# One decoder layer on one core: the first weight block and x^T arrive in fewer, larger transfers, and TensorE warms up with nine matmuls

## The chip, the core and the metric

The kernel runs on one core of a Trainium2 chip. The metric is device time in microseconds (us), from the start to the end of one execution; of several runs the median is given.

## What is computed

A decoder layer for 256 tokens of width 1024, in float32. Cut to what matters:

```python
proj = jnp.einsum('bsd,de->bse', x, w_in[l])                 # 1024 -> 3072
dq, dk, dv, mq, mk, mv = jnp.split(proj, splits, axis=-1)
a_out = diff_attention(dq, dk, dv, diff_lambda[l], diff_subln_g[l], lambda_init, cos, sin)
b_out = moba_attention(mq, mk, mv, cos, sin)
mix = jnp.einsum('bse,ed->bsd', jnp.concatenate([a_out, b_out], axis=-1), w_o[l])
x = layer_norm(ALPHA * x + mix, ln1_g[l], ln1_b[l])
g, u = jnp.split(jnp.einsum('bsd,df->bsf', x, w_ffn_in[l]), 2, axis=-1)
x = layer_norm(ALPHA * x + jnp.einsum('bsf,fd->bsd', jax.nn.silu(g) * u, w_ffn_out[l]), ln2_g[l], ln2_b[l])
```

## The kernel before

All weights stream through the core once, as 49 units of 1 MB: a unit is a tile of 128 partitions by 4 blocks of 512 columns. Six pairs of units belong to the input projection, four units to the output projection, 22 and 11 to the two layers of the FFN. A unit is loaded on SyncE's queue (SP) into `raw`, then split: ScalarE (ACT) rounds it to float32r into `hi` (L190 for unit 0, L106 for later ones), and VectorE (DVE) subtracts, `lo = raw - hi` (L192, L108; one piece of units 2 to 9 goes to GpSimd). x^T, eight blocks of 128 partitions by 256 tokens, is split in the same way into `xTh` and `xTl` (L178, L179). Each product of the projections is then three matmuls on TensorE (PE): hi by hi (L142), `xTl` by hi (L143) and `xTh` by lo (L144).

The projection walks over eight blocks of the contraction, block k of x^T with block k % 4 of unit 0 (k below 4) or unit 1 (k from 4). For one block, four output slices `pj_0` to `pj_3` take three matmuls of 256 columns each, 12 in all. So 48 matmuls need unit 0 and the first four blocks of x^T, and the next 48 need unit 1 and the last four.

The order of the start is written out by hand: the transfers in L182 to L189, the casts and subtractions in the loop at L190 to L192. While nothing has landed, PE runs WARM matmuls of 512 columns on a zeroed tile (L154). The loads of units 1 to 3 come behind it, in four pieces each (L95). SP issues one transfer after another, and a transfer whose completion counter is still in use by the eighth transfer before it waits for that one. Within these lists the tool that builds the program sets each engine's own order, so a change of the start can shift instructions further down.

```python
for i in range(4):
    nc.scalar.copy(hi[0][:, i, :], raw[0][:, i, :])
    split_x(i, i + 1, nc.vector.tensor_copy if i == 0 else nc.scalar.copy)
    nc.vector.tensor_sub(lo[0][:, i, :], raw[0][:, i, :], hi[0][:, i, :].bitcast(F32))
```

Of the kernel before, what the change touches and what calls it, by code (L numbers as in the profile page):

```python
# [27 lines left out]
ALPHA = 2.0 ** 0.25  # L28
LAMBDA0 = 0.8 - 0.6 * math.exp(-0.3 * 0)
EPS = 1e-5  # L30
WARM = 7


LOAD_PIECES = {1: 4, 2: 4, 3: 4, 4: 4, 5: 4, 6: 2, 7: 2}
# [22 lines left out]
def hybrid_layer_kernel(ctx, tc, xT, xr, w_in, w_o, w_f1, w_f2, cols, rows, lamb, rot, tri, out):  # L57
    nc = tc.nc
# [11 lines left out]
    units = []  # L70
# [11 lines left out]
    raw, hi, lo = {}, {}, {}  # L82
# [69 lines left out]
    wps = psB.tile([P, 512], F32, tag="b", name="wps")  # L152
    for i in range(WARM):
        nc.tensor.matmul(wps, warm[:, :P], warm, start=True, stop=True)  # L154
# [15 lines left out]
    def load_x(a, b):  # L170
        nc.sync.dma_start(xTr[:, a:b, :], xT[:, a:b, :])

    def load_w0(i):
        nc.sync.dma_start(raw[0][:, i, :], units[0][:, i, :])

    def split_x(a, b, copy=nc.scalar.copy):
        s = slice(a, b)
        copy(xTh[:, s, :], xTr[:, s, :])  # L178
        nc.vector.tensor_sub(xTl[:, s, :], xTr[:, s, :], xTh[:, s, :].bitcast(F32))  # L179

    load_w0(0)
    load_x(0, 1)  # L182
    load_x(1, 2)
    load_w0(1)
    load_x(2, 4)
    load_w0(2)
    load_w0(3)
    load_x(4, 8)
    for i in range(4):  # L189
        nc.scalar.copy(hi[0][:, i, :], raw[0][:, i, :])  # L190
# [648 lines left out]
```

## Time and profile before

| | |
|---|---|
| median of 3 runs | 315.06 us (314.43 to 316.19) |
| the profiled execution | 314.95 us |
| its span, first to last instruction | 313.2 us |
| busy share: PE, DVE, ACT, GpSimd | 96%, 81%, 57%, 12% |
| mean granted TensorE clock | 0.991 |

The span is what the trace covers; 1.75 us of the execution lie around it. Times in the rows below count from the span's start. A PE that counts as busy is not at its peak, since a matmul's recorded length overlaps the next one; the pace is the distance between two starts. An engine's idle time costs something only where the chain that ends last goes through it.

### The profile page before, as it was taken

Reading aid. Unit: us, or ns where it says so; the run is one execution under the profiler, and the core shown is the slowest. Engines: PE = TensorE matmul, PEld = TensorE weight load, DVE = VectorE, ACT = ScalarE, POOL = GpSimd, SP = SyncE. Lnnn points to the kernel's source line nnn. Section 1 sums busy time; section 2 is a strip of 40 time slices with the busy share of each in tenths; the row PEclk is TensorE's granted clock in tenths of the full one; section 3 lists DMA queues with packets and bytes.
Section 4 is the critical chain, followed back from the end, with each engine's and each line's share of the span. In section 5 each row is a group of like instructions: output and inputs, shape, how many; then the busy total and the mean of one; then the engine's idle time right before and its main releaser. Section 6 shows DMA issues by size and latency. Waiting matters only on the chain.

```text
span 313.2 us, 4707 instructions
## 1 busy us (share of the span) xinstructions
PE 300.7 (96%) x1726; PEld 256.2 (82%) x1726; DVE 254.3 (81%) x475; ACT 177.6 (57%) x346; POOL 36.3 (12%) x38
## 2 busy tenths in 40 slices
PE   8899899999999999999999999999999999999990
PEld 5799789867887788888888888888888888888880
DVE  3799999999977189939587797597778799897975
ACT  4767479488686228337367477457747665546000
POOL 1066653310030010200000000000000000000011
PEclk9999999999999999999999999999999999999996
DMA  6989943433466450576834744654561317642011
GB/s 185 375 287 340 422 173 136 134 137 134 135 213 218 186 190 19 191 330 222 314 105 165 268 148 143 248 194 151 195 223 47 134 41 282 215 157 113 0 67 67
DMA packets 13749, 57.17 MB, mean 183 GB/s; under 512 B 1664, under 2 KB 2432, under 8 KB 8864
## 3 DMA queue, kind: packets, MB, share of 16 engines
q1 hardware_dynamic: 13440, 54.79, 50.0%
q0 software_dynamic: 288, 2.10, 1.8%
q8 instruction: 13, 0.21, 0.3%
q14 instruction: 8, 0.07, 0.1%
HBM read 55.84 MB, written 1.05 MB: 182 GB/s over the span
## 4 chain that ended last, share of the span: by engine, by line
PE 76%; DVE 12%; DMA 4%; issue 3%; POOL 1%; ACT 1%; SPq 1%; DVEq 0%; ACTq 0%
PE fc L601 21%; PE foc L683 13%; PE fc L602 11%; PE fo L683 4%; DVE lo L108 4%; DMA raw<-in_w_in_dram 4%; PE wo L142 3%; PE fr L143 2%; PE fr L142 2%; PE wo L144 2%; PE wo L143 2%; PE fr L144 2%; PE pj L142 2%; PE pj L144 2%; PE pj L143 2%
## 5 line engine op out<-in xcount | busy, mean ns | idle before, releaser
L108 DVE TENSOR_TENSOR lo<-raw,hi 128x512 fp32r<-128x512 f32 (+2 forms) x108 | 105.5, 1001 | 21.4 <-ACT hi L106 21.3
L106 ACT CAST hi<-raw 128x512 fp32r<-128x512 f32 (+2 forms) x116 | 90.2, 826 | 21.9 <-PE wo L144 9.9
L601 PE MATMUL fc<-x1T,hi 128*128 128x512 f32 x288 | 100.1, 392 | 0.0
L602 PE MATMUL fc<-x1T,lo 128*128 128x256 f32 x288 | 80.5, 280 | 0.0
L601 PEld LDWEIGHTS fc<-x1T,hi 128*128 128x128 f32 x288 | 54.1, 188 | 11.9
L602 PEld LDWEIGHTS fc<-x1T,lo 128*128 128x128 f32 x288 | 54.0, 188 | 0.0
L142 PE MATMUL pj<-xTh,hi 128*128 128x256 f32 x128 | 36.7, 294 | 1.4 <-ACT hi L190 1.4
L144 PE MATMUL pj<-xTh,lo 128*128 128x256 f32 x128 | 36.0, 288 | 0.6 <-DVE lo L108 0.5
L143 PE MATMUL pj<-xTl,hi 128*128 128x256 f32 x128 | 36.5, 287 | 0.0
L604 ACT COPY v<-fc 128x256 f32<-128x256 f32 x36 | 13.3, 370 | 23.7 <-PE fc L602 23.6
L142 PEld LDWEIGHTS pj<-xTh,hi 128*128 128x128 f32 x128 | 24.3, 193 | 2.9 <-ACT hi L190 2.5
L144 PEld LDWEIGHTS pj<-xTh,lo 128*128 128x128 f32 x128 | 24.3, 193 | 1.3 <-DVE lo L108 0.7
L143 PEld LDWEIGHTS pj<-xTl,hi 128*128 128x128 f32 x128 | 24.6, 193 | 0.1
L605 DVE TENSOR_TENSOR v<-v,fc 128x256 f32<-128x256 f32 x36 | 15.0, 418 | 9.7 <-ACT v L604 9.6
L512 POOL TENSOR_TENSOR rsf<-rsf,mhalf 128x1 f32<-128x1 f32 x2 | 1.8, 924 | 175.8 <-DVE rsf L511 175.8
L683 PE MATMUL foc<-lo,hTh 128*128 128x512 f32 x52 | 20.5, 395 | 0.0
L683 PE MATMUL foc<-hi,hTl 128*128 128x512 f32 x52 | 20.5, 394 | 0.0
L683 PE MATMUL foc<-hi,hTh 128*128 128x512 f32 x52 | 20.5, 394 | 0.0
L108 POOL TENSOR_TENSOR lo<-raw,hi 128x512 fp32r<-128x512 f32 x8 | 13.8, 1720 | 20.4 <-ACT hi L106 20.4
L284 ACT ACTIVATE E<-E,negm 128x128 f32<-128x128 f32 (+1 forms) x32 | 14.2, 445 | 2.5 <-DVE negm L281 2.4
L247 POOL TENSOR_TENSOR sh<-sh,cs_sb 128x256 f32<-128x256 f32 (+1 forms) x12 | 13.3, 1124 | 18.2 <-DVE sh L245 17.5
L142 PE MATMUL pj<-hi,xTh 128*128 128x512 f32 x32 | 13.7, 428 | 0.0
(189 smaller groups left out, 553.3 us busy)
## 6 DMA issues: line engine op xcount, KB each, us to landing
raw<-in_w_f_dram SPq DMA_DIRECT2D x28, 1024.0 KB, 5.2
raw<-in_w_in_dram SPq DMA_DIRECT2D x24, 256.0 KB, 5.4
raw<-in_w_in_dram SPq DMA_DIRECT2D x4, 1024.0 KB, 6.3
raw<-in_w_o_dram SPq DMA_DIRECT2D x4, 1024.0 KB, 4.8
raw<-in_w_f_dram SPq DMA_DIRECT2D x10, 256.0 KB, 3.8
raw<-in_w_f_dram SPq DMA_DIRECT2D x5, 512.0 KB, 5.1
raw<-in_w_in_dram SPq DMA_DIRECT2D x4, 512.0 KB, 8.7
rows<-in_rows_dram POOLq DMA_DIRECT2D x2, 1024.0 KB, 6.6
```

The lines of the kernel that those rows point to most:

```text
L106: nc.scalar.copy(h[:, s, :], r[:, s, :])
L108: eng.tensor_sub(l[:, s, :], r[:, s, :], h[:, s, :].bitcast(F32))
L142: nc.tensor.matmul(ps, sh, mh, start=first, stop=False)
L143: nc.tensor.matmul(ps, sh, ml, start=False, stop=False)
L144: nc.tensor.matmul(ps, sl, mh, start=False, stop=last)
L247: nc.gpsimd.tensor_mul(sh, sh, sin2[:, :m, :])
L284: nc.scalar.activation(e, e, AF.Exp, bias=negm[g][:, i, u : u + 1], scale=-1.0, accum_out=ls[g][:, i, u : u + 1])
L601: nc.tensor.matmul(ps, hi[u][:, i, ws], x1T[:, k], start=k == 0, stop=False)
L602: nc.tensor.matmul(ps[:, 0, :], lo[u][:, i, ws], x1T[:, k, 0, :], start=False, stop=k == KT - 1)
L604: nc.scalar.copy(v, ps[:, 1, :])
L605: nc.vector.tensor_add(v, v, ps[:, 0, :])
L683: nc.tensor.matmul(bank[name] if ps is None else ps, x, w[:, cs], start=key not in opened, stop=last and (m, i) == (len(todo) - 1, 2))
```

## The change

Unit 0 is loaded in two transfers of two blocks (512 KB) instead of four of one block (256 KB). x^T comes in pieces of 2, 2 and 4 blocks instead of 1, 1, 2 and 4. The order is weight, x, weight, x, x. WARM goes from 7 to 9. The casts and subtractions keep their sizes and their order in the source.

```diff
-WARM = 7
+WARM = 9
...
-    def load_w0(i):
-        nc.sync.dma_start(raw[0][:, i, :], units[0][:, i, :])
+    def load_w0(a, b):
+        nc.sync.dma_start(raw[0][:, a:b, :], units[0][:, a:b, :])
...
-    load_w0(0)
-    load_x(0, 1)
-    load_x(1, 2)
-    load_w0(1)
+    load_w0(0, 2)
+    load_x(0, 2)
+    load_w0(2, 4)
     load_x(2, 4)
-    load_w0(2)
-    load_w0(3)
     load_x(4, 8)
```

SP, the start of the program. `raw_101` (now `raw_103`) is unit 0, the next two `raw` tiles are units 1 and 2. Before:

```order
L174 DMA raw_101<-in_w_in_dram 128x512
L171 DMA xTr<-in_xT_dram 128x256 x2
L174 DMA raw_101<-in_w_in_dram 128x512
L171 DMA xTr<-in_xT_dram 128x512
L174 DMA raw_101<-in_w_in_dram 128x512 x2
L171 DMA xTr<-in_xT_dram 128x1024
L95 DMA raw_139<-in_w_in_dram 128x512 x4
L95 DMA raw_144<-in_w_in_dram 128x512 x4
```

Now:

```order
L174 DMA raw_103<-in_w_in_dram 128x1024
L171 DMA xTr<-in_xT_dram 128x512
L174 DMA raw_103<-in_w_in_dram 128x1024
L171 DMA xTr<-in_xT_dram 128x512
L171 DMA xTr<-in_xT_dram 128x1024
L95 DMA raw_138<-in_w_in_dram 128x512 x4
L95 DMA raw_143<-in_w_in_dram 128x512 x4
```

Five transfers stand ahead of unit 1 where eight stood; the bytes are the same.

DVE, the start of the program. `lo_103` (now `lo_105`) belongs to unit 0. Before:

```order
L178 CAST xTh<-xTr 128x256
L192 TENSOR_TENSOR lo_103<-raw_101,hi_102 128x512
L179 TENSOR_TENSOR xTl<-xTr,xTh 128x256 x2
L192 TENSOR_TENSOR lo_103<-raw_101,hi_102 128x512
L179 TENSOR_TENSOR xTl<-xTr,xTh 128x256 x2
L192 TENSOR_TENSOR lo_103<-raw_101,hi_102 128x512 x2
L179 TENSOR_TENSOR xTl<-xTr,xTh 128x512 x2
```

Now:

```order
L189 TENSOR_TENSOR lo_105<-raw_103,hi_104 128x512
L178 CAST xTh<-xTr 128x256
L189 TENSOR_TENSOR lo_105<-raw_103,hi_104 128x512
L179 TENSOR_TENSOR xTl<-xTr,xTh 128x256 x2
L189 TENSOR_TENSOR lo_105<-raw_103,hi_104 128x512 x2
L179 TENSOR_TENSOR xTl<-xTr,xTh 128x256 x2
L179 TENSOR_TENSOR xTl<-xTr,xTh 128x512 x2
```

The first cast of x^T now stands behind the first subtraction of unit 0, and the first `xTl` behind the second one. ACT's order changes alike: both casts of a pair of weight blocks now stand ahead of the x block, then the second pair, then the next two x blocks.

PE, the first matmuls on unit 1 (`hi_186` and `lo_187`, now `hi_185` and `lo_186`). Before:

```order
L142 MATMUL pj_3_185<-xTh,hi_186 128x256
L143 MATMUL pj_3_185<-xTl,hi_186 128x256
L144 MATMUL pj_0_182<-xTh,lo_187 128x256
L144 MATMUL pj_1_183<-xTh,lo_187 128x256
L144 MATMUL pj_2_184<-xTh,lo_187 128x256
```

Now:

```order
L142 MATMUL pj_0_181<-xTh,hi_185 128x256
L143 MATMUL pj_0_181<-xTl,hi_185 128x256
L144 MATMUL pj_0_181<-xTh,lo_186 128x256
L142 MATMUL pj_1_182<-xTh,hi_185 128x256
L143 MATMUL pj_1_182<-xTl,hi_185 128x256
```

Before, eight matmuls on `hi` ran ahead of the first on `lo`; now the first on `lo` is the third.

## Rows read from the trace of the kernel before

**Rows 1.** The page's busy time and chain that ended last, whole span.

```profile
PE 300.7 (96%) x1726; PEld 256.2 (82%) x1726; DVE 254.3 (81%) x475; ACT 177.6 (57%) x346; POOL 36.3 (12%) x38
...
PE 76%; DVE 12%; DMA 4%; issue 3%; POOL 1%; ACT 1%; SPq 1%; DVEq 0%; ACTq 0%
```

**Rows 2.** The chain in order of time, first 20 us: start us, us, what.

```profile
3.53 6.57 DMA raw<-in_w_in_dram
10.12 6.01 DMA raw<-in_w_in_dram
```

**Rows 3.** Timeline of PE, first 14 us: start us, us, engine, line, operation, idle before.

```profile
1.19 3.17 PE L154 MATMUL wps<-warm 128*128 128x512 bf16 x7 [1.19 <-DVE tbl L150]
...
4.32 1.19 PE L142 MATMUL pj<-xTh,hi 128*128 128x256 f32 x4
...
6.75 0.41 PE L143 MATMUL pj<-xTl,hi 128*128 128x256 f32 x1
...
7.12 0.28 PE L142 MATMUL pj<-xTh,hi 128*128 128x256 f32 x1
7.24 0.28 PE L143 MATMUL pj<-xTl,hi 128*128 128x256 f32 x1
...
10.12 0.39 PE L142 MATMUL pj<-xTh,hi 128*128 128x256 f32 x1 [1.42 <-ACT hi L190]
...
13.20 0.33 PE L142 MATMUL pj<-xTh,hi 128*128 128x256 f32 x1
```

**Rows 4.** Busy time by stretch; the last numbers are granted clock, DMA share, GB/s.

```profile
5.00:10.00 5.00, 3.70 (x23) 3.42 (x22) 2.12 (x5) 2.29 (x5) 0.00 (x0) 1.00 0.83 258
10.00:15.00 5.00, 4.88 (x39) 4.81 (x40) 4.28 (x7) 4.22 (x9) 0.00 (x0) 1.00 1.05 392
```

**Rows 5.** Timeline of SP's queue, first 15 us: issues of transfers.

```profile
0.74 0.37 SPq L174 DMA_DIRECT2D raw<-in_w_in_dram  x1
1.17 0.89 SPq L171 DMA_DIRECT2D xTr<-in_xT_dram  x2
...
4.48 9.97 SPq L95 DMA_DIRECT2D raw<-in_w_in_dram  x12
```

**Rows 6.** Transfers 1, 3, 4, 5, 7, 8, 9: KB, us from issue to landing.

```profile
raw<-in_w_in_dram SPq DMA_DIRECT2D x1, 256.0 KB, 2.8
...
xTr<-in_xT_dram SPq DMA_DIRECT2D x1, 128.0 KB, 3.3
...
raw<-in_w_in_dram SPq DMA_DIRECT2D x1, 256.0 KB, 3.6
...
xTr<-in_xT_dram SPq DMA_DIRECT2D x1, 256.0 KB, 5.2
...
raw<-in_w_in_dram SPq DMA_DIRECT2D x1, 256.0 KB, 6.6
...
xTr<-in_xT_dram SPq DMA_DIRECT2D x1, 512.0 KB, 7.4
...
raw<-in_w_in_dram SPq DMA_DIRECT2D x1, 256.0 KB, 7.6
```

**Rows 7.** Timeline of ACT, first casts of a weight block and of x^T.

```profile
3.57 0.62 ACT L190 CAST hi<-raw 128x512 fp32r<-128x512 f32 x1 [1.33 <-DMA raw<-in_w_in_dram]
...
5.01 0.41 ACT L178 CAST xTh<-xTr 128x256 fp32r<-128x256 f32 x1 [0.82 <-DMA xTr<-in_xT_dram]
```

**Rows 8.** Timeline of DVE, its first three operations on data.

```profile
3.88 0.29 DVE L178 CAST xTh<-xTr 128x256 fp32r<-128x256 f32 x1 [2.74 <-DMA xTr<-in_xT_dram]
4.22 0.69 DVE L192 TENSOR_TENSOR lo<-raw,hi 128x512 fp32r<-128x512 f32 x1
4.83 0.42 DVE L179 TENSOR_TENSOR xTl<-xTr,xTh 128x256 fp32r<-128x256 f32 x1
```

**Rows 9.** Timeline of PE, 30 to 40 us: two waits for DVE.

```profile
34.33 0.39 PE L144 MATMUL pj<-xTh,lo 128*128 128x256 f32 x1 [0.52 <-DVE lo L108]
...
39.17 0.38 PE L143 MATMUL s<-l,h 64*128 64x256 f32 x1 [0.45 <-DVE l L254]
```

## The prediction

> **What bounds the kernel now.** I read the page first. PE is busy for 96% of the span, and three quarters of the chain that ended last are PE's [rows 1]. So what the start of the kernel gives to PE, and what is not lost again before PE takes over for good, comes out of the time one for one. The chain in order of time says what the start hangs on: from 3.53 to 16.13 us it is nothing but weight transfers [rows 2]. The timeline of PE shows the same from its side [rows 3]: seven warming matmuls from 1.19 to 4.36, the first real matmul at 4.32, a hole of 1.42 us that ends at 10.12 when block 2 of unit 0 has been cast, and the first matmul on unit 1 at 13.20. Behind that PE waits for DVE at 34.33 (0.52 us) and at 39.17 (0.45 us) [rows 9]; between 5 and 10 us it stands for 1.30 us in 5 [rows 4].
>
> The pace of PE in rows 3 needs a word. Seven matmuls of 512 columns start 0.42 apart (3.17 us for all, the last one's tail included), which is 1.2 GHz; 256 columns at that level take 0.21. From about 7.0 us on, 256 columns take 0.12, which is 2.4 GHz. So the rise came 5.8 us after PE's first matmul, and PE had been at work almost without a break until then. The granted clock of these stretches reads 1.00 throughout [rows 4], so the rise is read from the pace alone.
>
> The transfers: SP issues one every 0.47 us, from 0.74 on, and reaches unit 1 at 4.48 [rows 5]. The times to landing grow from 2.8 to 7.6 us [rows 6], so the pieces land at 3.54 (block 0 of unit 0), 4.97 (x 1; x 0 a little over 3.8, since DVE casts it at 3.88 [rows 8]), 5.7 (block 1), 7.8 (x 2 and 3), 10.1 (block 3), 11.4 (x 4 to 7) and 12.1 (first piece of unit 1). The rate is 258 GB/s between 5 and 10 us and 392 from 10 to 15 [rows 4]. The start is short of bytes, and bytes move slower there than later.
>
> **The change, part by part.** The bytes and all compute instructions stay, but for two warming matmuls. What changes is when blocks land, and in which order ACT and DVE take them.
>
> *Issues.* Five transfers instead of eight stand ahead of unit 1. By 0.47 us each they are issued at 0.74, 1.2, 1.7, 2.1 and 2.6, and unit 1 follows at 3.1 instead of 4.48. SP loses nothing by it.
>
> *First weight pair, 512 KB.* Its first half cannot be used before the second has landed. Landing: not before 3.54 + 0.67 = 4.2, which is the landing of 256 KB plus another 262 kB at 392 GB/s; not after 4.97, when the same number of bytes had landed before in three pieces. I take 4.3, near the fast end, because it is one transfer and not three. The Trainium skill, page "DMA: Bandwidth & Descriptors", section "Anatomy of one DMA — SWDGE (gpsimd) path", speaks against this part: the completion fires only when the last byte has landed, after about 2.0 us and the bytes at 436 GB/s. That would put the pair at 0.74 + 2.0 + 1.2 = 3.9 and a single block at 3.3, an estimate from that page, where the trace has 3.54 for the single block. By it the first real matmul would come at 5.6 and not at the 6.0 worked out below, two more matmuls would be done by 7.0, and the end would be 0.2 us earlier.
>
> *x 0 and 1, 256 KB.* 4.3 plus 0.75 (between 0.67 at 392 GB/s and 1.02 at 258) is 5.05; bounds 4.9 and 5.7.
>
> *ACT.* A cast of a weight block takes 0.62, of an x block 0.41 [rows 7]. Blocks 0 and 1: 4.34 to 4.96 to 5.58; x 1: to 5.99.
>
> *DVE.* This is where the new order costs. The cast of x 0 stands behind the first subtraction, the first `xTl` behind the second. A subtraction takes 0.69, with starts 0.61 apart (4.22 to 4.83), an `xTl` 0.42, the cast 0.29 [rows 8]. From 4.98: `lo` 0 to 5.63, x 0 cast to 5.93, `lo` 1 to 6.55, `xTl` 0 to 6.95, `xTl` 1 to 7.35.
>
> *PE.* The first real matmul at 5.98, against 4.32. The nine warming matmuls end at 1.19 + 9 x 0.427 = 5.03, so the two that are added lie in a wait and cost nothing; they would cost up to 0.85 us only if data were there at 4.2, which the landing above excludes. PE stands still for about 0.95 us. The four matmuls on `xTh` run to 6.83, the next waits for `xTl` 0 until 7.0. If the clock is up by then, the remaining 8 of block 0 take 0.95 and the 12 of block 1 1.43: 9.4.
>
> *Second weight pair and x 2 and 3.* 512 KB more at 258 GB/s are 2.03: 7.1. Bounds 6.2 (392 GB/s) and 10.1 (when block 3 landed before). x 2 and 3 one more 1.02: 8.1. ACT casts blocks 2 and 3 from 7.1 to 8.4, x 2 and 3 to 9.2. DVE, behind it, has `xTl` 2 and 3 by about 9.5 and 9.9. PE comes at 9.4 and finds block 2 nearly ready, then block 3: 24 matmuls at 0.12 are 2.86, so unit 0 is done at 12.3, against 13.20. In other words: at 7.0 PE has done 4 matmuls where it had done 12, which puts it 0.95 behind at the fast pace; in return the hole of 1.42 and smaller halts of 0.45 (from 7.0 to 13.20, less the hole and 36 matmuls at 0.12) go. That is 0.9.
>
> *x 4 to 7 and unit 1.* At 258 GB/s x lands at 10.1 (bounds 8.2, and 11.4 as before), the first piece of unit 1 at 10.9 (8.9 and 12.1). DVE subtracts x 4 to 7 to about 12.05 and the first `lo` of unit 1 to 12.7. In the new order the third matmul on unit 1 needs it, at 12.3 + 0.24, so PE waits 0.15 there. **Net 0.75 us.**
>
> *Afterwards.* The transfers of units 1 and 2 are about 1.1 us earlier, and with them ACT and DVE, so PE's waits for DVE at 34 and 39 us stay about as long as they were: DVE's lead over PE grows by 0.3 at most, and I count nothing. DVE and GpSimd take some subtractions and shuffles up to 80 us in another order; with no row for that I bound it by half a wait of rows 9 either way, 0.25, and take nothing.
>
> The sum, against the profiled execution: 314.95 - 0.75 = **314.2**. The median of the runs shown is 315.06, 0.11 higher.
>
> **The rivals.**
>
> *The clock comes up late (slower).* PE's work is broken for about 1 us just before the rise. If the rise is then as far behind the new beginning as it was behind the first, 5.8 us, it comes at 11.8. Block 0 ends at 8.7 (8 matmuls at 0.213 from 7.0), block 1 at 11.3, 2 matmuls more at 11.8, 10 at 0.12 to 13.0, block 3 at 14.4. That is 1.2 us later than 13.20: **316.1**. It decides from the point where PE's hole is long enough to undo the seven or nine warming matmuls; against it speaks that a hole of 1.42 us at 8.7 did not bring the slow pace back [rows 3], though that was after the rise. The Trainium skill, page "TensorE: Matmul & The Clock Gate", section "Why this matters for your kernels", asks for unbroken work until the clock is up; the trace agrees with it so far, since the rise followed 5.8 us of nearly unbroken work.
>
> *The whole load runs at the later rate (faster).* If the 258 GB/s came from many small transfers, and the larger ones run at 392, the second pair lands at 6.2, x 4 to 7 at 8.2, unit 1 at 8.9. PE is then held by its own start alone: unit 0 at 12.3 as before, but no wait for `lo` (0.9 gained), and DVE is over 1 us further ahead of PE than now, which takes away the two waits of rows 9, 0.97: 314.95 - 1.87 = **313.1**.
>
> *Hidden anyway.* If x 4 to 7 still land at 11.4, DVE's stream is where it was; PE is 0.9 us early on unit 0 and waits 0.9 longer for `lo` of unit 1 or at 34 us: **315.0**. For it: the chain of rows 2 is all transfers, and the bytes are the same.
>
> **How the numbers follow.** My forecast 0.43, the late clock 0.22, the full rate 0.20, hidden 0.15. About 0.5% (1.6 us) is what a measurement of this kernel can tell from no change. Only the full rate reaches that on the fast side: nearly all of its 0.20, and 0.03 of the forecast's edge, 0.23. On the slow side the late clock gives 1.2 and needs 0.4 more, from a first pair at 4.97 or the new order further down: 0.10. The rest, 0.67, is within. The range goes from 312.8, the full rate with 0.25 for the order further down, to 316.2, the late clock.
>
> **What would show it.** Right: first transfer landed at about 4.3, first real matmul near 6.0 with a hole of about 1 us before it, no hole around 9 us, the pace of 0.12 from about 7 us, the first matmul on unit 1 near 12.3. The late clock: a pace of 0.21 beyond 9 us. The full rate: near 390 GB/s between 5 and 10 us. Hidden: the matmul on unit 1 early, and longer waits for DVE behind it. My forecast is wrong if the first pair lands after 5 us or if PE is not done with unit 0 before 13.2.

## The result, and the profile of the changed kernel

The changed kernel takes 318.71 us (median of 4 executions, 318.07 to 319.00) against 315.04 us (4 executions, 314.43 to 316.19): 1.0107 times as long, 95% interval 1.0079 to 1.0135. The forecast was 314.2 with a range to 316.2, so the prediction was wrong, in sign too. The profiled execution took 318.52 us with a span of 316.7: 3.5 us more span than before.

Its page, busy time and the chain that ended last, beside [rows 1]:

```profile
PE 301.4 (95%) x1728; PEld 256.0 (81%) x1728; DVE 253.3 (80%) x475; ACT 177.5 (56%) x346; POOL 35.1 (11%) x38
...
PE 79%; DVE 12%; issue 2%; ACT 2%; DMA 2%; POOL 1%; SPq 0%; DVEq 0%; ACTq 0%; POOLq 0%
```

PE's busy sum rose by 0.7 us only; the time in which it stood grew from 12.5 to 15.3 us. Transfers went from 4% of the chain to 2%: it leaves them at 8.7 us now and at 16.1 before, so the start hangs less on them, as meant. Yet PE's timeline of the start (columns as in [rows 3]) reads:

```profile
1.19 4.02 PE L154 MATMUL wps<-warm 128*128 128x512 bf16 x9 [1.19 <-DVE tbl L150]
6.59 0.71 PE L142 MATMUL pj<-xTh,hi 128*128 128x256 f32 x4 [1.38 <-ACT xTh L178]
7.43 0.38 PE L143 MATMUL pj<-xTl,hi 128*128 128x256 f32 x1
...
10.20 0.39 PE L142 MATMUL pj<-xTh,hi 128*128 128x256 f32 x1
11.04 0.38 PE L143 MATMUL pj<-xTl,hi 128*128 128x256 f32 x1 [0.45 <-DVE xTl L179]
...
13.86 0.28 PE L142 MATMUL pj<-xTh,hi 128*128 128x256 f32 x1
```

The first real matmul starts at 6.59 after a hole of 1.38 us, not at 5.98 after 0.95. The fast pace is there at once (four matmuls in 0.71 us), and the hole ahead of block 2 is all but gone. Unit 1 begins at 13.86, 0.66 later than the 13.20 of [rows 3], where the sum had it at 12.3. The transfers of these blocks (KB, us from issue to landing) are issued on SP at 0.74, 1.18, 1.65 and 2.11:

```profile
raw<-in_w_in_dram SPq DMA_DIRECT2D x1, 512.0 KB, 4.1
...
xTr<-in_xT_dram SPq DMA_DIRECT2D x1, 256.0 KB, 5.0
...
raw<-in_w_in_dram SPq DMA_DIRECT2D x1, 512.0 KB, 7.0
...
xTr<-in_xT_dram SPq DMA_DIRECT2D x1, 256.0 KB, 7.3
```

So they land at 4.9, 6.2, 8.7 and 9.4. ACT's casts of the weight pairs show it (beside [rows 7]), and SP's row shows when unit 1 joins in (beside [rows 5]):

```profile
4.90 1.14 ACT L187 CAST hi<-raw 128x512 fp32r<-128x512 f32 x2 [2.66 <-DMA raw<-in_w_in_dram]
...
8.70 1.14 ACT L187 CAST hi<-raw 128x512 fp32r<-128x512 f32 x2 [2.14 <-DMA raw<-in_w_in_dram]
```

```profile
3.43 10.27 SPq L95 DMA_DIRECT2D raw<-in_w_in_dram  x12
```

**Where the 3.5 us are.** I laid each matmul of the changed kernel beside the same one of the kernel before, by its place in PE's stream, and took the difference of their starts, called the lag here. It is +0.6 from 14 to 32 us, between -0.1 and +0.5 to 57 us, +1.2 from 58 to 65 us (a longer wait for `E`, the probabilities of the first attention; it is given back) and +0.55 from 66 to 70 us. At 71 us it jumps to +1.90, and from 74 us on it is +3.4 to the end. So some 0.55 is lost ahead of 70 us. It is not simply the start's 0.6 carried along: that is made up by 34 us, and at 38.80 PE waits 0.62 us for ACT's cast `h`, where it waited 0.06 before. Nearly all the rest is lost in one place of 4 us, where the last projection pieces and the first scores of the second attention meet. PE's timeline there:

```profile
70.41 0.40 PE L144 MATMUL pj<-hi,xTl 128*128 128x512 f32 x1
71.85 0.35 PE L142 MATMUL s<-h,h 64*128 64x256 f32 x1 [1.05 <-DVE negm L278]
72.37 0.38 PE L143 MATMUL s<-l,h 64*128 64x256 f32 x1 [0.16 <-DVE l L251]
...
73.69 0.80 PE L142 MATMUL pj<-hi,xTh 128*128 128x512 f32 x1
74.28 0.63 PE L143 MATMUL pj<-lo,xTh 128*128 128x512 f32 x1
...
75.99 0.63 PE L144 MATMUL pj<-hi,xTl 128*128 128x512 f32 x1
76.55 0.59 PE L142 MATMUL s<-h,h 64*128 64x256 f32 x2
```

The kernel before goes through the same instructions without a wait and without a slow stretch:

```profile
69.85 0.40 PE L144 MATMUL pj<-hi,xTl 128*128 128x512 f32 x1
70.18 0.38 PE L142 MATMUL s<-h,h 64*128 64x256 f32 x1
70.46 0.38 PE L143 MATMUL s<-l,h 64*128 64x256 f32 x1
...
71.79 0.51 PE L142 MATMUL pj<-hi,xTh 128*128 128x512 f32 x1
...
73.39 0.39 PE L142 MATMUL s<-h,h 64*128 64x256 f32 x2
```

Two losses can be read off. From the last projection matmul to the second score matmul 1.96 us go by (70.41 to 72.37) where it was 0.61 (69.85 to 70.46): 1.35 us of **waiting**. Then six matmuls of 512 columns take 2.86 us (73.69 to 76.55) where they took 1.60, and the scores behind them lose another 0.23: 1.5 us of **slow pace**. The windows of PE say what this pace is; the number after the five engines' busy times is the granted clock, which is 1.00 here in the kernel before:

```profile
72.00:73.00 1.00, 0.78 (x5) 0.38 (x5) 1.00 (x6) 0.89 (x5) 0.00 (x0) 1.00 1.08 131
73.00:74.00 1.00, 1.00 (x8) 0.88 (x9) 1.00 (x6) 0.83 (x4) 0.00 (x0) 0.84 0.87 369
74.00:77.00 3.00, 3.00 (x10) 1.96 (x11) 3.00 (x17) 2.55 (x13) 0.00 (x0) 0.50 0.43 183
77.00:78.00 1.00, 1.00 (x12) 0.84 (x11) 1.00 (x2) 0.90 (x5) 0.00 (x0) 0.95 0.00 0
```

It is 0.50, the 1.2 GHz level, through 74 to 77 us and a little on both sides, right behind the place where PE had stood.

**Why PE waits there.** The score matmul at 71.85 waits until DVE has read earlier scores (it takes the negated row maximum, `negm`, from them), the one at 72.37 for `l`. `h` and `l` are the rounded part and the remainder of the queries and keys, as `hi` and `lo` are of the weights. On DVE `negm` and `l` both stand behind the rope (the rotation of queries and keys by their position) of projection 3's second half, which begins with a shuffle. DVE in the kernel before, from the first half's rope addition on:

```profile
62.91 0.68 DVE L251 TENSOR_TENSOR a<-a,sh 128x512 f32<-128x512 f32 x1
63.51 1.28 DVE L108 TENSOR_TENSOR lo<-raw,hi 128x512 fp32r<-128x512 f32 x2
64.71 0.68 DVE L254 TENSOR_TENSOR l<-a,h 128x512 fp32r<-128x512 f32 x1
...
65.32 0.73 DVE L245 STREAM_SHUFFLE sh<-pj 128x512 f32<-128x512 f32 x1
...
69.73 0.68 DVE L254 TENSOR_TENSOR l<-a,h 128x512 fp32r<-128x512 f32 x1
```

And in the changed kernel:

```profile
63.47 0.68 DVE L248 TENSOR_TENSOR a<-a,sh 128x512 f32<-128x512 f32 x1
64.07 0.68 DVE L108 TENSOR_TENSOR lo<-raw,hi 128x512 fp32r<-128x512 f32 x1
64.89 0.69 DVE L251 TENSOR_TENSOR l<-a,h 128x512 fp32r<-128x512 f32 x1
65.72 0.69 DVE L108 TENSOR_TENSOR lo<-raw,hi 128x512 fp32r<-128x512 f32 x1
66.61 0.69 DVE L108 TENSOR_TENSOR lo<-raw,hi 128x512 fp32r<-128x512 f32 x1 [0.20 <-ACT hi L106]
...
67.23 0.74 DVE L242 STREAM_SHUFFLE sh<-pj 128x512 f32<-128x512 f32 x1
...
71.63 0.68 DVE L251 TENSOR_TENSOR l<-a,h 128x512 fp32r<-128x512 f32 x1
```

From the shuffle to `l` it is 4.41 us before and 4.40 now. From the addition to the shuffle it was 2.41 us and is now 3.76, 1.35 more, which is PE's loss: before, `l` was done at 70.41 and PE took it at 70.46, so there was no slack. A third subtraction stands ahead of the shuffle (0.61), and DVE halts three times, 0.22, 0.23 and 0.28 us beyond the 0.60 between starts, each time until a cast of ACT ends (the first at 64.24 + 0.62 = 64.86). ACT is late because its order changed too. Before, it did a weight cast at 60.76, while the addition was not ready; now that cast stands behind the cast `h` of the addition's result, and ACT idles instead:

```profile
60.76 0.62 ACT L106 CAST hi<-raw 128x512 fp32r<-128x512 f32 x1 [0.60 <-PE pj L144]
63.67 0.62 ACT L253 CAST h<-a 128x512 fp32r<-128x512 f32 x1 [2.29 <-DVE a L251]
```

```profile
64.24 0.62 ACT L250 CAST h<-a 128x512 fp32r<-128x512 f32 x1 [2.91 <-DVE a L248]
```

Nothing in the source changed there. The tool that builds the program sets each engine's order, and with the first weight blocks arriving as a pair it set DVE, ACT and GpSimd differently in some 40 places between about 17 and 93 us.

### The profile page after: what moved, and what is told of

It reads as the page before. It is cut to its first block, busy times and chain, and to the rows that moved or that the text cites. A ratio compares the mean times of both kernels' runs of the same rounds, so it can differ in the third digit from the quotient of the medians.

```text
span 316.7 us, 4704 instructions
## 1 busy us (share of the span) xinstructions
PE 301.4 (95%) x1728; PEld 256.0 (81%) x1728; DVE 253.3 (80%) x475; ACT 177.5 (56%) x346; POOL 35.1 (11%) x38
## 3 DMA queue, kind: packets, MB, share of 16 engines
HBM read 55.84 MB, written 1.05 MB: 180 GB/s over the span
## 4 chain that ended last, share of the span: by engine, by line
PE 79%; DVE 12%; issue 2%; ACT 2%; DMA 2%; POOL 1%; SPq 0%; DVEq 0%; ACTq 0%; POOLq 0%
PE fc L598 21%; PE foc L680 13%; PE fc L599 11%; PE fo L680 4%; DVE lo L108 4%; PE pj L142 3%; PE pj L143 3%; PE pj L144 3%; PE wo L142 2%; PE fr L143 2%; PE fr L142 2%; PE wo L143 2%; PE wo L144 2%; PE fr L144 2%; DMA raw<-in_w_in_dram 2%
## 5 line engine op out<-in xcount | busy, mean ns | idle before, releaser
L244 POOL TENSOR_TENSOR sh<-sh,cs_sb 128x256 f32<-128x256 f32 (+1 forms) x12 | 13.1, 1106 | 12.3 <-DVE sh L242 12.3
```

Of the source, the lines that this page charges most:

```text
L244: nc.gpsimd.tensor_mul(sh, sh, sin2[:, :m, :])
```

## The experiments

The theories when the first runs were sent: **A**, the order further down costs, by itself; **B**, the late start costs, and what is seen at 71 us follows from it; **C**, the order makes the wait, and the slow pace of the clock comes on top of it by a chance of the execution or from a second cause. To hold an order fixed, some kernels carry it as a table, `ORDER`, one row of instruction numbers for each of DVE, ACT and GpSimd; at the end a function ties each instruction to the one before it on its engine, without a semaphore:

```diff
+ORDER = [
+    [55, 66, 80, 91, 107, 137,
...
+    def pin_order():
...
+        for numbers in ORDER:
+            for a, b in zip(numbers, numbers[1:]):
+                tc.add_manual_dep(named[f"I-{first + b}"], f"I-{first + a}",
...
+    pin_order()
```

All results in one table. The runs of before beside them had medians of 314.90 to 315.09; the ratio is to those.

| kernel | executions | median (range), us | ratio, 95% interval |
|---|---|---|---|
| e1 new start, old order | 10 | 316.10 (315.65 to 316.54) | 1.0014 [0.9991, 1.0037] |
| e2 old start, new order | 10 | 317.02 (316.08 to 318.55) | 1.0061 [1.0037, 1.0085] |
| e3 changed kernel, hole filled | 10 | 317.69 (316.49 to 318.81) | 1.0066 [1.0038, 1.0093] |
| e4 changed kernel, 7 warming | 5 | 318.33 (317.56 to 318.88) | 1.0086 [1.0053, 1.0119] |
| e5 changed kernel, old order late | 5 | 316.16 (316.00 to 317.24) | 1.0035 [1.0004, 1.0065] |
| e6 only x 0 and 1 merged | 10 | 315.78 (315.02 to 316.95) | 1.0020 [0.9998, 1.0043] |
| e7 only second pair merged | 10 | 315.97 (314.98 to 317.56) | 1.0029 [1.0005, 1.0052] |
| e8 changed kernel, second pair split | 4 | 319.01 (318.30 to 319.09) | 1.0123 [1.0108, 1.0138] |
| e9 only two more warming | 10 | 314.92 (314.39 to 315.64) | 0.9988 [0.9966, 1.0010] |
| e10 only the late order | 11 | 317.76 (315.62 to 319.27) | 1.0061 [1.0029, 1.0092] |
| e11 one subtraction moved | 12 | 315.53 (315.15 to 317.41) | 1.0022 [0.9997, 1.0046] |
| e12 as e9, again | 12 | 315.17 (314.23 to 316.94) | 1.0012 [0.9988, 1.0037] |

(A twelfth execution of e10 took 595.71 us and is left out of its row. The recorded ratio is not the quotient of the two medians.)

The mean granted clock is on record for every execution, and helps to read the ranges. Of the 92 executions of the kernel before beside these runs, 76 took at most 315.69 us, with a mean clock of 0.991 to 0.996; 16 took over 316.5, with 0.988 to 0.990, and are 2.0 us longer in the mean. The profiles tell what this is: the clock is at 0.50 in the last microseconds of all 14, and the four with a mean of 0.990 or less (the changed kernel, e8, e10, e11) are the four in which it also fell earlier; the ten with 0.991 or more have no such fall. So I read a mean of 0.990 or less as such a fall. Where it lay only a profile tells.

### e1 and e2: start and order apart

e1 is the changed kernel with the old order of DVE, ACT and GpSimd behind the start; e2 is the kernel before with the new one. Both are the `ORDER` table above with the other kernel's numbers.

> The changed start, with VectorE, ScalarE and GpSimd tied, from the first instruction behind the start on, to the order that they had before. If the order further down costs the 3.4 us (theory A), the lag of 0.6 us that the start leaves at 14 us is taken back by about 36 us as in the changed kernel, no slow pace appears at 74 us, and the time is 314.5 to 315.5. If the late start itself costs them, because it leaves VectorE no reserve (theory B), the lag opens again at 70 us and the time stays at 317.5 to 319.

> The start of before, with VectorE, ScalarE and GpSimd tied, from the first instruction behind the start on, to the order of the changed kernel. Theory A: the same halts between 57 and 77 us, the slow pace behind them, and 317 to 318.7. Theory B: 315 to 315.5. If both parts are needed (theory C), the halts are there but TensorE keeps its fast pace, and the time is 315.5 to 317.

e1's median lies 1.0 us over before's, though the interval of the ratio includes 1, and over the 314.5 to 315.5 that A gave; its profile has the first real matmul at 6.69, a lag of +0.5 from 33 us to the end, which is not taken back as A's text had it, and no jump at 71 us. e2, with the old start, shows the jump in full: the lag goes from -0.2 to +1.14 in front of this row,

```profile
71.10 0.35 PE L148 MATMUL s<-h,h 64*128 64x256 f32 x1 [1.04 <-DVE negm L287]
```

but its profile has no slow pace behind it. So the order costs by itself and B falls for the bulk: the wait appears without the late start, and is gone with the old order in spite of it. The wait of 0.6 us for `h` near 38 us is there in e2 too (0.59), so it also comes with the order. The profile of e2 is what its text gives for C. Its ten executions split by the clock: six with a mean of 0.992 to 0.995 took 316.08 to 317.21, four with 0.988 to 0.990 took 317.78 to 318.55. So the order is worth some 1.7 us without a fall of the clock, and some 1.5 more where the clock falls, which it does in part of the executions. The start alone is worth some 0.5 to 1.0 us.

### e3: what the hole does to the clock

The changed kernel, orders tied, with six matmuls on a zeroed tile added to an open sum where PE would stand:

```diff
+            if (c, n) == (4, SCORES1[2]):
+                for _ in range(6):
+                    nc.tensor.matmul(pss[t], warm[:, :P], warm, start=False, stop=False)
```

> The changed kernel, orders tied, with six matmuls of 512 columns of zeros added to an open sum just before the third pair of scores of the second head group, where TensorE stands still for over 1 us at 70.6 us. They take 6 x 0.215 = 1.3 us at the fast pace. If the slow pace from 73.7 to 77.1 us comes from that standstill, it is gone, and 1.3 to 1.6 us with it, less what the six take beyond the wait (0.1 to 0.3): 317.1 to 317.5. If it does not hang on it, the time is 318.7 to 319.

The six fill the wait (five are in the records), and the projection matmuls behind run at the fast pace, 0.34 and 0.23 apart as before:

```profile
72.65 1.24 PE L428 MATMUL pj<-warm 128*128 128x512 bf16 x5
73.83 0.38 PE L148 MATMUL s<-h,h 64*128 64x256 f32 x1
...
75.47 0.50 PE L148 MATMUL pj<-hi,xTh 128*128 128x512 f32 x1
75.81 0.39 PE L149 MATMUL pj<-lo,xTh 128*128 128x512 f32 x1
```

The scores still come 1.35 late: filling changes no order. The profiled execution itself was long (318.81) because the first rise of the pace came only at 12.9 us. The median is 1.0 us under the changed kernel's, but five of the ten executions (317.60 to 317.91) have a mean clock of 0.987 to 0.989, as the changed kernel's have: the clock fell in them in spite of the filling, in a place that no profile shows. e2 had no slow pace either with the hole unfilled. So e3 does not show that filling keeps the pace up.

### e4: the warming matmuls

The changed kernel with `WARM = 7`.

> The changed kernel with seven warming matmuls instead of nine; the orders are the same. The two hide in the wait for the first pair. If they keep the pace up at the start, TensorE's pace rises later without them, the first blocks run at 0.21 per matmul, and unit 1 begins 1 to 2 us later than 13.9; in the end 318.7 to 320. If they do nothing: 318.7.

The median is 0.4 under the changed kernel's, within the spread. The jump at 71 us is there (1.34), the slow pace behind it is not, and the first rise came at 10.5 us. So late a rise comes with nine matmuls too (e3, e5). The two matmuls are not what costs.

### e5: the order behind 60 us alone

The changed kernel with its own order up to about 61 us; behind that, from the first half's `l` of projection 3 on, DVE (place 103) and ACT (place 75) take the old one.

> The changed kernel with its own order up to about 61 us; only from the subtraction of the third projection's first query half on do VectorE and ScalarE stand in the order of before. What this undoes on VectorE is small: one subtraction of a weight piece that the changed kernel has ahead of the shuffle of the second half's queries and keys goes behind it again, and the places that follow from it. If that one place makes TensorE wait at 70.6 us, the 1.34 us there and the slow pace behind it are gone: lag about 0.6 us from 66 us to the end, 315.5 to 316.2. If the order before 61 us is what leaves VectorE late, the wait stays: 317 to 318.7.

The wait and the slow pace are gone in the profile. Between the projection and the scores PE's timeline has the distances of before again, 0.32 and 0.29:

```profile
71.97 0.40 PE L150 MATMUL pj<-hi,xTl 128*128 128x512 f32 x1
72.29 0.38 PE L148 MATMUL s<-h,h 64*128 64x256 f32 x1
72.58 0.38 PE L149 MATMUL s<-l,h 64*128 64x256 f32 x1
```

The median falls from 318.71 to 316.16, as far as e1's; e8, below, ran beside it with the changed order and took 319.01. The profiled execution is the longest of the five (317.24): its lag is +2.1 from 66 us to the end, not the 0.6 of the text, because the first rise of the pace came only at 12.7 us. So of the 40 places those behind 60 us, fewer than half, carry the 2.5 us, and those ahead nothing that these runs can tell.

### e6, e7, e8: which transfer it is

e6 and e7 are the kernel before with one part of the change each, e8 the changed kernel with the second pair split again.

```diff
 e6
-    load_x(0, 1)
-    load_x(1, 2)
+    load_x(0, 2)
 e7
-    load_w0(2)
-    load_w0(3)
+    load_w0(2, 4)
 e8
-    load_w0(2, 4)
     load_x(2, 4)
+    load_w0(2, 3)
+    load_w0(3, 4)
```

> Before, with x 0 and 1 in one transfer; seven warming matmuls, unit 0 in four transfers. VectorE, ScalarE and GpSimd keep the order of before. The theory that the order costs most: no halt at 70 us, and only the start moves, by the later landing of x 0 (about 4.6 instead of 3.84, so the first matmul near 4.9 instead of 4.32); 314.7 to 315.6. If any merged piece makes the start late by itself: 316 to 316.5.

> Before, with only blocks 2 and 3 of unit 0 in one transfer, behind x 2 and 3; seven warming matmuls. The orders of before stay. Block 3 landed at 10.1 in the kernel before and block 2 at 9.4; as one transfer both come between 9.0 and 10.1, so PE's hole of 1.4 us is about as long as it was: 314.7 to 315.5. It would be 313.5 to 314.5 only if the merged transfer moved faster than the two.

> The changed kernel with blocks 2 and 3 of unit 0 in two transfers again, behind x 2 and 3. The first pair alone already gives VectorE, ScalarE and GpSimd the changed order. If the order is what costs, this is as slow as the changed kernel, 317.5 to 319; if the second pair has a part in it, 315.5 to 316.5.

e6 and e7 keep the old order further down and cost 0.7 and 0.9 in the median, lags of +0.3 and +0.2 in their profiles. Both medians lie a little over the range that was given for them (by 0.2 and 0.5), and e6's interval includes 1. In e7 PE's wait in front of block 2 grew from the 1.42 of [rows 3] to 1.90: block 2 began 0.30 later, since it now waits for block 3's bytes, and PE was done 0.19 earlier in front of it. e8 has the changed kernel's order and all of its loss: lag +0.4 at 68 us, +1.8 at 71 and +3.3 from 77 us. So the merged first pair (with the x transfers as in the change) brings the new order with it, and the second pair adds nothing to it. Which rule of the building tool moved the instructions was not tried.

### e9 and e12: two more warming matmuls

The kernel before with `WARM = 9`, twice.

> The kernel before with nine warming matmuls instead of seven, nothing else changed. The ninth ends at about 5.0 us where data are there at 4.3, so if data alone set the first real matmul before, it now comes near 5.05, 0.73 later. What of that reaches the end: the hole in front of block 2 (1.42 us) takes it up, so theory A (the cost lies further down) expects 315.0 to 315.4; if every delay of the start reached the end, 315.8.

> The kernel before with nine warming matmuls, as e9 once more, for the spread of its executions: in e9 ten of ten lay between 314.39 and 315.64, while 14 of the 75 executions of the kernel before that ran beside the experiments lay above 316.5. If the two matmuls take that upper group away, none of about twelve lies above 316.5 here and the mean is some 0.3 us below that of the kernel before; if they do nothing, about two of twelve lie above it. The median should be 314.8 to 315.2 by either theory.

They cost nothing that can be measured. The first matmuls come 0.3 to 0.7 later in e9's profile, and the lag is 0.0 from block 3 on: the wait in front of block 2 shrank from 1.42 to 0.84. That the two matmuls keep executions from lying above 316.5, as e9 let hope, did not hold: 4 of 12 did in e12, all four with a mean clock of 0.989 or 0.990, 4 of 22 in both, and 16 of 92 of the kernel before.

### e10 and e11: the place alone, and one subtraction

e10 is the kernel before with the new order on DVE and ACT behind 60 us only, the counterpart of e5. e11 moves one number of DVE's row and leaves ACT and GpSimd as they were:

```diff
-746, 809, 723, 794, 795, 814, 818
+746, 809, 723, 814, 794, 795, 818
```

> The kernel before with its own order on VectorE and ScalarE up to about 60 us, and from there on the order of the changed kernel (VectorE from place 103, ScalarE from place 75). Theory A (the one place behind 60 us costs): PE waits some 1.1 us for negm near 71 us, 316.2 to 316.6, and up to 1.5 us more where the pace falls behind that wait. Theory B (the place costs only where the start is late): 315.0 to 315.3.

> The kernel before with one instruction of VectorE moved: the fourth subtraction of the weights in front of the rope of projection 3's second half stands ahead of the shuffle instead of two places behind it; ScalarE and GpSimd as before. Theory A in its narrow form (this one subtraction makes the second half late): the shuffle 0.6 to 0.8 later, the wait for negm at 71 us 0.5 to 0.8, 315.6 to 316.0, and up to 1.5 more where the pace falls. If ScalarE's order is what makes it late: 315.0 to 315.2.

e10's profile has the wait, 1.42 us, and a jump of the lag of 1.7:

```profile
72.97 0.35 PE L148 MATMUL s<-h,h 64*128 64x256 f32 x1 [1.42 <-DVE negm L287]
```

Five of its executions lie between 315.6 and 316.4, about 1.0 over before's median, with a mean clock of 0.993 or 0.994; six lie between 317.8 and 319.3, with 0.985 to 0.989. The place is therefore enough to cost, and B falls here too. In the profiled one, 318.09 us, the pace fell in the start as well, behind a wait of 1.76 us in front of block 2:

```profile
8.00:11.00 3.00, 1.24 (x10) 0.96 (x9) 1.77 (x4) 1.56 (x4) 0.00 (x0) 1.00 0.96 313
11.00:14.00 3.00, 3.00 (x16) 3.00 (x16) 2.37 (x5) 2.67 (x6) 0.00 (x0) 0.50 1.05 398
```

Against the kernel before that cost 1.5 us; there was no fall behind 71 us. e11 makes the shuffle 0.8 late and costs 0.38 at 71 us in the profile, 0.5 in the median (the interval includes 1), just under what the narrow form of A expected. Half of the 0.8 comes back, because the place behind the shuffle stays empty and the rope's addition follows it by 2.21 us instead of 2.65; in the changed kernel another subtraction stands there, and it is 2.64. The one subtraction is thus a part. That the larger part comes with ACT's later casts, which e10 has and e11 has not, is what the rows of DVE and ACT above say; e10 moves other instructions too, so these two runs alone do not show it.

## Why the prediction was wrong

**The step that failed is "Afterwards": the order further down, bounded by 0.25 us either way and taken as 0.** It measured 1.35 us of waiting, and 1.5 us of slow pace behind it in the profiled execution (1.7 and some 1.5 by e2's executions). The bound came from half a wait of [rows 9], which are two waits of subtractions; the order was known to move up to 80 us, but what stands in it was not followed. The difference of the orders, set beside the rows of DVE and ACT at 60 to 72 us, would have shown a shuffle that PE needs going behind another subtraction, in a stretch in which DVE is busy without a break: one subtraction is 0.6, beyond the bound already. Nor does the range hold the bound on its slow side: 316.2 is the late clock alone, while 312.8 has the 0.25 in it.

**The landings were second.** They turned the forecast gain of 0.9 at the end of unit 0 into a loss of 0.66. The first pair came at 4.9 in place of 4.3, near the bound 4.97: one transfer of 512 KB gained nothing on three pieces. The estimate of 3.9 that the prediction drew from the Trainium skill is off by 1.0; the section that it names is on transfers issued by GpSimd, and these are issued by SyncE. x 0 and 1 came at 6.2 (5.05, bound 5.7), the second pair at 8.7 (7.1). The rate was not at fault, it was better than taken:

```profile
4.90:8.70 3.80, 2.29 (x15) 1.80 (x15) 2.17 (x5) 1.54 (x4) 0.00 (x0) 1.00 0.97 309
```

In these 3.8 us 1.17 MB moved, while x 0 and 1 and the second pair together are 0.79 MB. By these bytes alone, in order, they would have landed by 7.4. So at least 0.38 MB belonged to transfers issued later. The trace tells where the rest of the time went: each transfer raises its completion counter in 16 steps, and of the second pair's 16 the first came at 6.29, the fourteenth at 7.64 and the last two at 8.31 and 8.67. The sum took a transfer to land as a whole when its bytes are through; it lands with its slowest share, here 1.0 us behind the fourteenth. The last two shares of x 2 to 7 and of unit 1's first piece come 0.5 and 0.8 behind their fourteenth as well. By the Trainium skill, page "DMA: Bandwidth & Descriptors", section "Issuing engines are not separate DMA queues", transfers run on the same 16 DMA engines and interleave, whichever engine issued them. The trace agrees for transfers of one queue: the first share of x 2 and 3 was there at 7.02, 1.65 us before the second pair was complete. Whether the two late shares would have come sooner with less issued behind them is not shown; no run held unit 1 back. A slip in the sum had no weight: by its own rate the first piece of unit 1 lands at 11.1, not at 10.9.

**What followed from the landings.** The first real matmul was to start at 5.98 and started at 6.59; unit 0 was done 0.66 later than before instead of 0.9 earlier. The parts in between were right in kind: ACT's and DVE's order, the hole of PE behind nine warming matmuls (1.38, 0.95 forecast), no hole of 1.4 in front of block 2. A wait of 0.45 for `xTl` of block 2 stands in its place, which the sum did not have. The two warming matmuls lay in a wait, as said; e4, e9 and e12 fit it.

**The rivals.** The full rate did not come: over 5 to 10 us 335 GB/s moved against 258 in [rows 4], but it went to all transfers at once. Hidden did not come either, since unit 0 was done late and not early. The late clock, at the start, did not come in the profiled execution of the change, where the pace was fast at 6.6 us; that is luck, since with the same nine warming matmuls and the same first transfer it stayed slow to 9.6 in e8, 12.7 in e5 and 12.9 in e3, around the 11.8 that the rival gave. With it the lag at 20 us was +1.9 in e5 and +2.1 in e3, against +0.6 here. So the rival was worth more than its 0.22. Its mechanism, a hole in PE's work that costs the pace, took effect at 73 us, where the prediction did not look. The Trainium skill, page "TensorE: Matmul & The Clock Gate", section "Why this matters for your kernels", warns of drops in mid-kernel behind long gaps between bursts of matmuls; the trace shows the drop behind less than the Trainium skill names there, a wait recorded as 1.05 us with thin work around it.

**The ledger** of the profiled execution: ahead of 70 us 0.55, waiting 1.35, slow pace 1.5, sum 3.4 of lag, of the 3.5 in the span. By medians: e1 1.0 for the start (316.10 against 315.07), and e5 takes 2.55 away with the place behind 60 us; together 3.6 of 3.67.

## What to carry to other kernels

Where a tool sets the order of the instructions, a change of transfers at the start is also a change of order far behind it: compare the orders of the two programs over the whole length, and for each moved instruction look up in the trace who waits for what stands behind it. A merged transfer delays its first half to the landing of its second, and a transfer counts as landed only with its slowest share, so bytes over rate gives too early a time. A stop of PE of 1 us can cost more than itself, since the pace may fall behind it.

## What the runs showed of the hardware that was not expected

The time of the first rise differs between executions of like starts: by the pace it came at 7.0 us in the kernel before, at 6.6 or earlier in the changed one, at 9.6 in e8, at 12.7 in e5 and at 12.9 in e3, after the same nine warming matmuls in all but the first. The granted clock reads 1.00 while that slow pace lasts. What PE did before it sorts the profiles. In seven PE went from the warming matmuls to the first real one without a hole of 0.3 us or more (before, e2, e7, e9 to e12), and the pace was up by 7.1 us or earlier in all of them. In the other seven it stood for 1.2 to 2.2 us there; in two of these the pace was up with the first real matmul (the changed kernel, e1), in five it came only at 9.6 to 12.9 (e3, e4, e5, e6, e8).

Later falls do show in the granted clock: 0.50 at 74 to 77 us in the changed kernel, at 75 to 78 in e8, at 11 to 14 in e10 and at 12 to 15 in e11. Each lay behind a wait of PE of 1.05 to 2.11 us with thin work around it, but a like wait at 71 us left the pace alone in e2, e4 and e10, and waits of 1.90 and 1.77 in front of block 2 did so in e7 and e12. So what the profiles show is that such a wait can bring the fall, not that it must. Either event is worth about 1.5 to 2 us.

The 16 executions of the kernel before above 316.5 are of this kind by their mean clock of 0.988 to 0.990, against 0.991 to 0.996 in the 76 others; none of them was profiled, so where the clock fell is open. All four executions of the changed kernel have 0.988 or 0.989, the profiled one among them, which fits a fall in each of them; that it lay behind 71 us is shown for the one that was profiled.
